# Group norm of a recurrent mixer with eight fused VectorE operations and an early table load, and a new table of how much other work goes into each wait

## The chip, the cores and the metric

The kernel runs on one core of a Trainium2 chip. The metric is the time of one execution on the device in microseconds (us). Engines are called PE (TensorE), VectorE (DVE), ScalarE (ACT), GpSimd (POOL) and SyncE (SP, which issues the DMAs).

## The reference, cut to what matters

One layer over 256 latent tokens of width 1024 with 256 context tokens. A combined input projection feeds two mixers: a recurrence in two directions (8 heads of 64, first over the context, then over the latents) and a windowed attention. Their outputs are projected, gated, merged and projected back; then comes a mixture of 16 experts. The change touches what follows the recurrence:

```python
def rwkv_out(y, r, k, v, lg, r_k, g_lora_b, ln_g, ln_b, out_dtype):
    mu = jnp.mean(y, axis=-1, keepdims=True)                 # per head, over 64
    var = jnp.mean(jnp.square(y - mu), axis=-1, keepdims=True)
    yn = ((y - mu) * lax.rsqrt(var + GN_EPS)).reshape(bsz, t, D_A) * ln_g.astype(f) + ln_b.astype(f)
    bonus = (jnp.sum(r * k * r_k.astype(f), axis=-1, keepdims=True) * v).reshape(bsz, t, D_A)
    g = jax.nn.sigmoid(lg.astype(f)) @ g_lora_b.astype(f)
    return ((yn + bonus) * g).astype(out_dtype)
```

and the router's scores: `scores = sigmoid(t @ router_w)`.

## The kernel before, in words

**Stages in time (profile of before).** Input, modulation and first projections to about 72 us; first preparation (`rw_prep(0)`, decays and products for the context) to 131; first triangular solve (`rw_solve`, 62 small VectorE operations) to 170; first pass (`rw_chain(0)`, 8 rounds over blocks of 32 tokens) to 246; second preparation (`rw_prep(1)`, for the latents) to about 335; second solve to 376; second and last pass (`rw_chain(1)`, rounds 0 to 7) to 437.6; group norm to 454; projections of the two mixers and output projection to 496; router to 502.7; experts to the end.

**Critical work and other work.** The recurrence is a chain of short steps on PE, VectorE and ScalarE with waits between them. The "other work" is one long Python generator, `others()`: value projection, attention, the receptance, the gates, and the projections of the attention's output. `fill()` takes the next number of the list `FILL` (156 numbers, one for each call, the last is 698, "all that is left") and advances the generator by so many steps. Most steps are three matmuls (128x128 weights, 256 columns); the attention's steps are its own pieces, every second or fourth step beside a projection is one of them, and the last two steps of each output group of `gates_b` have 12 matmuls each. Counted through the code the generator has 437 steps: values 65, first attention projection 66, attention of the first half beside the second projection 92, receptance 32, attention of the second half 38, gates 72, `gates_b` 72. `until(name)` advances it until a named point: "v" (66 steps) before the first solve, "r" (256) after the first pass, "att" (294) in the second preparation. Its splits of weights (`split`, L280 on ScalarE, L281 on VectorE) belong to it.

**Order.** The framework's planner puts the instructions of each engine in an order at compile time, from dependencies and its own cost table; among instructions that it takes to be ready, the one that stands earlier in the program goes first. Other work that is ready may therefore be issued ahead of its place in the program when PE would wait. The products in `warm` (L275; bf16, results unused) are kept behind the last matmul of the critical work by edges without a wait, `tc.add_manual_dep(..., ORDERED)`. All DMAs go through SP's queue.

**The group norm** (L1154 to L1184), y being 4 blocks Q of 128x256, in two pairs i:

```python
for i in range(2):
    p = pb(); warm(p, ("gn", i)); mm(p, C["ob"], fl(y, i))            # sum over a head
    V.scalar_tensor_tensor(fl(y, i), p, -1.0 / 64, fl(y, i), ...)     # L1158: y - mean
    S.activation(fl(sq, i), fl(y, i), AF.Square)                      # L1159
fill()
... mm(p, C["obc"], sq) ...; rsqrt(rn.ap, p, 1.0 / 64, 64e-5)         # L285 VectorE, L286 Sqrt, L287 reciprocal
fill()
... pq[Q] = selp x rn, four PSUM banks ...
# then the lines that the change replaces, L1172 to L1176, and for each pair i:
#   five products of warm into a bank freed by the block before, four matmuls (gate),
#   L1181 y * gate (VectorE, PSUM), L1183 cast (ScalarE), L1184 y - cast (VectorE)
```

`rsqrt`'s Sqrt needs another activation table than Tanh and Exp; a table load (ACT_TABLE_LOAD) is put in front of the first activation that needs one. `pb()` and `pa()` hand out PSUM banks, four of each. At the end of the output projection L1272 (VectorE) and L1273 (Sqrt, ScalarE) form the norm of x1, L1275 copies the last quarter of x1 out of PSUM on ScalarE, L1290 forms the scores, L1291 is their Sigmoid, and L1382 a later copy on ScalarE.

Of the kernel before, what the change touches and what calls it, by code (L numbers as in the profile page):

```python
# [13 lines left out]
AF = mybir.ActivationFunctionType  # L14
ALU = mybir.AluOpType
# [103 lines left out]
def _pack(I):  # L119
# [40 lines left out]


FILL = [
# [4 lines left out]
]  # L167
ORDER = [(("k0", 1), ("k1", 0))] * 3

# [63 lines left out]
def hybrid_kernel(ctx: ExitStack, tc: tile.TileContext, a, out, dbg=None, stop=None):  # L233
    nc = tc.nc
    V, S, G, T = nc.vector, nc.scalar, nc.gpsimd, nc.tensor
# [15 lines left out]
    qpool, Q = region("arena_q", NQ, F32R)  # L251
# [5 lines left out]
    def pb(name="pb"):  # L257
        return ps.tile([128, 512], F32, tag="b", name=name, bufs=4)

    own, other = [None], [False]  # L260
    ORDERED = mybir.DependencyInfo(mybir.DependencyClass.NoSync, mybir.DependencyReason.DATA)
# [31 lines left out]
    W = {n: vec[:, o:o + w] for n, (o, w) in _VOFF.items()}  # L293
# [291 lines left out]
    for f in range(2):  # L585
        for q, p in enumerate(fout[f"k{f}"]):
            Q = 2 * f + q
# [276 lines left out]
    vf = A.get(4, 256)  # L864
# [260 lines left out]
    y = A.get(4, 256)  # L1125
# [12 lines left out]
    glb, late, x1 = A.get(512), A.get(128 + NCST[1]), A.get(2, D)  # L1138
# [7 lines left out]
    ssq, rs2, std, junk = A.get(2, 3), A.get(2), A.get(2), A.get(256)  # L1146
    tob = A.get(128)
    sco, sel, gate, gstd, one, oneb, s2 = [A.get(2, 16) for _ in range(7)]
# [2 lines left out]
    pos, over = A.get(2, 16), A.get(2)  # L1151
    ring_grow(A)
    fl = lambda b, i: b[:, 2 * i:2 * i + 2, :].rearrange("p q t -> p (q t)")
    for i in range(2):  # L1154
        p = pb()
        warm(p, ("gn", i))
        mm(p, C["ob"], fl(y, i))
        V.scalar_tensor_tensor(fl(y, i), p, -1.0 / 64, fl(y, i), op0=ALU.mult, op1=ALU.add)  # L1158
        S.activation(fl(sq, i), fl(y, i), AF.Square)  # L1159
# [7 lines left out]
    pq = [pb() for _ in range(4)]  # L1167
    for Q in range(4):
        warm(pq[Q], ("gn", 3), 256)
    for Q in range(4):  # L1170
        mm(pq[Q][:, 0:256], C["selp"][32 * Q:32 * Q + 32, :], rn[32 * Q:32 * Q + 32, :])
    for Q in range(4):  # L1172
        V.tensor_tensor(y[:, Q, :], y[:, Q, :], pq[Q][:, 0:256], op=ALU.mult)
        V.tensor_scalar(y[:, Q, :], y[:, Q, :], W["lng"][:, Q:Q + 1], W["lnb"][:, Q:Q + 1], op0=ALU.mult, op1=ALU.add)
    for i in range(2):
        G.tensor_tensor(fl(y, i), fl(y, i), fl(vf, i), op=ALU.add)  # L1176
        p = pb()
        warm(p, ("gn", 4 + i))
        for q in range(2):
            mm(p[:, q * 256:(q + 1) * 256], glb[:, (2 * i + q) * 128:(2 * i + q + 1) * 128], lg.ap)  # L1180
        V.tensor_tensor(fl(y, i), fl(y, i), p, op=ALU.mult)  # L1181
        yh, yl = ya[i]
        S.copy(yh.r.rearrange("p q t -> p (q t)"), fl(y, i))  # L1183
        V.tensor_tensor(yl.r.rearrange("p q t -> p (q t)"), fl(y, i), yh.ap.rearrange("p q t -> p (q t)"), op=ALU.subtract)  # L1184
# [51 lines left out]
    for n4 in range(4):  # L1236
# [13 lines left out]
        pv = p.rearrange("p (t c) -> p t c", t=2)  # L1250
# [21 lines left out]
    V.scalar_tensor_tensor(std.ap, pss[:, 0:32:16], 1.0 / D, rs2.ap, op0=ALU.mult, op1=ALU.add)  # L1272
    S.activation(std.ap, std.ap, AF.Sqrt)  # L1273
    V.reciprocal(rs2.ap, std.ap)
    S.copy(x1[:, :, 768:1024], pv)  # L1275
    A.put(*wraw, junk, rws)
    P.put(xT)
    ring_grow(P)
# [9 lines left out]

    for tt in range(2):
        V.scalar_tensor_tensor(sco[:, tt, :], plg[tt][:, 0:16], rs2[:, tt:tt + 1], l3.ap, op0=ALU.mult, op1=ALU.add)  # L1290
    S.activation(sco.ap, sco.ap, AF.Sigmoid)  # L1291
    rb = rb.ap.unsqueeze(1).to_broadcast([128, 2, 16])
    V.tensor_tensor(sel.ap, sco.ap, rb, op=ALU.add)

# [213 lines left out]
```

## Time and profile before

| | us |
|---|---|
| median of 3 runs | 741.64 (737.54 to 742.75) |
| profiled execution, its own time | 737.73 |
| its span | 735.9 |
| last pass of the recurrence | 376.0 to 437.6 |
| group norm up to the second split's end | 437.6 to 453.9 |

The span goes from the first to the last instruction; 1.8 us of the execution lie around it. Times in the rows are us from the span's start. "Lnnn" is the line of the kernel; for helpers (`mm` L264, `split` L280 and L281, `rsqrt` L285 to L287) it is the helper's. A wait at the end of a row is the idle time of that engine before the instruction and what ended it.

### The profile page before, as it was taken

What the parts mean: (1) busy time and instruction counts of PE and PEld (TensorE: products, weight loads), DVE (VectorE), ACT (ScalarE), POOL (GpSimd) and SP (SyncE); (2) the same over time, 40 slices, a digit from 0 to 9 for tenths busy, and PEclk for the clock granted to TensorE, in tenths of its full rate; (3) what the DMA queues carried; (4) which work ended last, traced back from release to release, by engine and by line L of the source; (5) the groups of instructions that cost most, each with busy time, mean ns of one, the idle gap of its engine ahead of it and who ended that gap; (6) DMA issues with size and microseconds to landing.
All of it is one profiled execution on the core that took longest, in us unless ns stands there. A gap on an engine that the chain in (4) does not pass through costs nothing.

```text
span 735.9 us, 14592 instructions
## 1 busy us (share of the span) xinstructions
PE 681.6 (93%) x6053; PEld 455.6 (62%) x6059; DVE 397.4 (54%) x738; ACT 301.4 (41%) x604; POOL 101.0 (14%) x90
## 2 busy tenths in 40 slices
PE   4999788999999979689999998998999999999996
PEld 2667677885777844367988766995534544544532
DVE  2445985999774586968975456844213212212113
ACT  5436677447755366845444423432201101101110
POOL 0002354003223044350012201000000000000000
PEclk9999879999999977999999999999999999999999
DMA  9844011231120343777651158969999999999951
GB/s 363 324 168 134 4 59 37 80 107 59 59 63 20 112 147 113 237 262 261 201 193 60 56 197 306 361 245 381 410 408 411 409 410 412 406 411 411 409 220 61
DMA packets 46297, 165.34 MB, mean 225 GB/s; under 512 B 5392, under 2 KB 6800, under 8 KB 45328
## 3 DMA queue, kind: packets, MB, share of 16 engines
q1 hardware_dynamic: 46224, 164.34, 59.9%
q8 instruction: 49, 0.80, 0.4%
q14 instruction: 24, 0.20, 0.1%
HBM read 163.27 MB, written 1.05 MB: 223 GB/s over the span
## 4 chain that ended last, share of the span: by engine, by line
PE 73%; DVE 12%; ACT 9%; issue 2%; DMA 2%; POOL 1%; DVEq 0%; ACTq 0%; POOLq 0%
PE pa L264 53%; PE pb L264 16%; DVE arena_q L281 3%; ACT arena L753 2%; ACT arena L736 1%; PE pb L275 1%; PE pa L967 1%; ACT arena_q L280 1%; DVE arena L696 1%; DVE arena L790 1%; DVE arena L792 1%; DMA arena<-in_modr_dram 1%; DMA arena<-in_pab_dram 1%; DVE arena L693 1%; PE pb L338 1%
## 5 line engine op out<-in xcount | busy, mean ns | idle before, releaser
L264 PE MATMUL pa<-arena_p,arena_q 128*128 128x256 f32 (+1 forms) x984 | 164.3, 314 | 3.3 <-ACT arena_p L373 1.2
L264 PEld LDWEIGHTS pa<-arena_p,arena_q 128*128 128x128 f32 x984 | 134.5, 189 | 24.1 <-issue 5.5
L264 PE MATMUL pa<-arena,arena_m 128*64 128x512 f32 (+1 forms) x652 | 147.1, 555 | 0.0
L264 PE MATMUL pb<-arena 128*32 128x64 f32 (+13 forms) x2248 | 112.0, 270 | 17.7 <-DVE arena L710 5.7
L264 PEld LDWEIGHTS pb<-arena 128*32 128x32 f32 (+7 forms) x2246 | 70.3, 137 | 54.7 <-issue 19.7
L264 PEld LDWEIGHTS pa<-arena,arena_m 128*64 128x64 f32 x652 | 48.5, 137 | 83.7 <-issue 80.3
L280 ACT CAST arena_q<-arena 128x1024 fp32r<-128x1024 f32 (+1 forms) x66 | 62.8, 955 | 80.9 <-PE pa L264 55.1
L281 DVE TENSOR_TENSOR arena_q<-arena,arena_q 128x1024 fp32r<-128x1024 f32 (+1 forms) x66 | 77.6, 1176 | 23.3 <-ACT arena_q L280 18.7
L1408 DVE TENSOR_TENSOR arena_m<-arena_m,pa 128x512 f32<-128x512 f32 x8 | 5.5, 688 | 96.7 <-PE pa L264 96.7
L264 PE MATMUL pa<-arena_q,arena_p 128*128 128x256 f32 x384 | 57.2, 296 | 0.0
L264 PEld LDWEIGHTS pa<-arena_q,arena_p 128*128 128x128 f32 x384 | 49.4, 194 | 6.3 <-issue 3.6
L813 POOL TENSOR_TENSOR arena<-arena 64x512 f32<-64x512 f32 x30 | 32.0, 1068 | 115.6 <-DVE arena L843 113.7
L1349 ACT ACTIVATE arena_m<-pa,arena 128x128 f32<-128x128 f32 x32 | 12.1, 457 | 78.0 <-PE pa L264 78.0
L264 PE MATMUL pa<-arena_p,arena_m 128*64 128x512 f32 x140 | 41.3, 593 | 0.0
L264 PE MATMUL pa<-arena 128*64 128x256 f32 (+5 forms) x192 | 37.8, 446 | 1.7 <-ACT arena L968 1.7
L280 ACT CAST arena_r<-arena_m 128x512 fp32r<-128x512 f32 x16 | 9.9, 618 | 64.9 <-DVE arena_m L1428 64.9
L1428 DVE SCALAR_TENSOR_TENSOR arena_m<-pa,arena,arena_p 128x512 f32<-128x512 f32 x16 | 12.0, 751 | 43.1 <-PE pa L264 43.1
L264 PEld LDWEIGHTS pa<-arena_m,arena 128*128 128x128 f32 x256 | 30.8, 201 | 6.6 <-issue 5.7
L809 ACT COPY arena<-arena 32x256 f32<-32x256 f32 x64 | 25.8, 403 | 18.7 <-PE pb L264 16.8
L264 PE MATMUL pa<-arena_m,arena 128*128 128x128 f32 x256 | 32.3, 287 | 0.9 <-DVE arena_m L1336 0.9
L843 DVE TENSOR_TENSOR arena<-pb,arena 64x512 f32<-64x512 f32 x30 | 20.7, 689 | 15.9 <-PE pb L264 15.4
L264 PE MATMUL pb<-arena,arena 64*64 64x64 f32 (+1 forms) x496 | 26.9, 251 | 0.7 <-ACT arena L829 0.6
(210 smaller groups left out, 846.2 us busy)
## 6 DMA issues: line engine op xcount, KB each, us to landing
arena<-in_w_dram SPq DMA_DIRECT2D x137, 512.0 KB, 9.6
arena<-in_win_dram SPq DMA_DIRECT2D x42, 512.0 KB, 4.0
arena_p<-in_w_dram SPq DMA_DIRECT2D x35, 512.0 KB, 10.1
arena<-in_modr_dram SPq DMA_DIRECT2D x32, 512.0 KB, 4.1
arena<-in_modw_dram SPq DMA_DIRECT2D x4, 2048.0 KB, 14.3
arena<-in_w_dram SPq DMA_DIRECT2D x20, 256.0 KB, 8.2
arena_m<-in_w_dram SPq DMA_DIRECT2D x10, 512.0 KB, 8.8
arena<-in_pab_dram SPq DMA_DIRECT2D x8, 512.0 KB, 3.2
```

The source lines that it names most:

```text
L264: i = T.matmul(out, lhsT, rhs, start=start, stop=stop, skip_group_check=True)
L275: i = T.matmul(p[:, 512 - n:], cb("ob", 128), cb("scanm", n), start=True, stop=True, skip_group_check=True)
L280: S.copy(dhi.bitcast(F32R), src)
L281: eng.tensor_tensor(dlo.bitcast(F32R), src, dhi, op=ALU.subtract)
L338: T.transpose(p[:, (2 * k + i) * 128:(2 * k + i + 1) * 128], xn[:, 2 * st + i, kc * 128:(kc + 1) * 128], ident)
L693: V.tensor_tensor_scan(cum[:, go], C["scanm"], sg[:, go], 0.0, op0=ALU.mult, op1=ALU.add)
L753: (V.tensor_copy if h and c2 else S.copy)(BT[f][64 - 64 * h:128 - 64 * h, d, q, c2:8:2, :], pv[64 * c2:64 * c2 + 64, :, h, :])
L809: S.copy(Z[rv, h, :, d, :], vt[32 * c4:32 * c4 + 32, h, tt, :, :])
L813: G.tensor_tensor(sd[r_], Z[r_, h], pc[r_, :, :, i].rearrange("p d q -> p q d").unsqueeze(3) .to_broadcast([64, 4, 2, 64]), op=ALU.mult)
L843: V.tensor_tensor(Z1[r_, h], pyv[r_], sd[r_], op=ALU.add)
L1349: S.activation(dst, src, AF.Identity, scale=m4[:, kc:kc + 1], bias=m3[:, kc:kc + 1])
L1428: V.scalar_tensor_tensor(sil.ap, py[n2], gsl[pr % 2].ap, m5r[:, n2 * 512:(n2 + 1) * 512], op0=ALU.mult, op1=ALU.mult)
```

## The change

Two activations stand ahead of the group norm; the scale and shift of each block are two `scalar_tensor_tensor` operations on VectorE, (y * ln_g) * rstd and (y + ln_b) + bonus, done for each pair of blocks inside the loop over pairs, and GpSimd's additions are gone; the copy L1275 is ordered behind the Sigmoid of the scores on ScalarE, by an edge without a wait; `FILL` has other numbers.

```diff
+    S.activation(std[:, 0:1], y[:, 0, 0:1], AF.Square)
+    S.activation(std[:, 0:1], std[:, 0:1], AF.Sqrt)
     for i in range(2):
         p = pb()
         warm(p, ("gn", i))
...
-    for Q in range(4):
-        V.tensor_tensor(y[:, Q, :], y[:, Q, :], pq[Q][:, 0:256], op=ALU.mult)
-        V.tensor_scalar(y[:, Q, :], y[:, Q, :], W["lng"][:, Q:Q + 1], W["lnb"][:, Q:Q + 1], op0=ALU.mult, op1=ALU.add)
     for i in range(2):
-        G.tensor_tensor(fl(y, i), fl(y, i), fl(vf, i), op=ALU.add)
+        for Q in (2 * i, 2 * i + 1):
+            V.scalar_tensor_tensor(y[:, Q, :], y[:, Q, :], W["lng"][:, Q:Q + 1], pq[Q][:, 0:256], op0=ALU.mult, op1=ALU.mult)
+        for Q in (2 * i, 2 * i + 1):
+            V.scalar_tensor_tensor(y[:, Q, :], y[:, Q, :], W["lnb"][:, Q:Q + 1], vf[:, Q, :], op0=ALU.add, op1=ALU.add)
         p = pb()
         warm(p, ("gn", 4 + i))
...
-    S.copy(x1[:, :, 768:1024], pv)
+    x1_last = S.copy(x1[:, :, 768:1024], pv)
...
-    S.activation(sco.ap, sco.ap, AF.Sigmoid)
+    scored = S.activation(sco.ap, sco.ap, AF.Sigmoid)
+
+    tc.add_manual_dep(x1_last.ins, scored.ins.name, ORDERED, reason="not before")
```

The numbers of `FILL` that differ, each with the wait that it belongs to (counted through the calls of `fill()`):

| where | old | new |
|---|---|---|
| first preparation: third wait of the products (half 0, direction 1); turn of half 0, direction 0 | 4; 0 | 3; 3 |
| first solve: after columns 21; 27 | 2; 2 | 1; 0 |
| first pass: round 3, start; round 4, second wait | 0; 0 | 3; 2 |
| second preparation: last turn of half 0, ahead of `until("att")` | 1 | 6 |
| second preparation, half 1: after the second decay; second and third wait of the products (direction 1) | 1; 3, 4 | 0; 2, 3 |
| second solve: after column 5 | 2 | 1 |
| last pass, round 0: third wait | 3 | 5 |
| round 1: second, third, fourth wait | 0, 2, 2 | 2, 3, 3 |
| round 2: second, third | 2, 7 | 3, 6 |
| round 5: second, third, fourth | 1, 6, 2 | 2, 9, 3 |
| round 6: second, third | 2, 10 | 3, 16 |
| round 7: second | 6 | 1 |

The sum without the last number is 312 in the old list and 330 in the new one.

## Rows read from the trace of the kernel before

**Rows 1.** The page, part 1 (busy time of each engine, its share of the span, and its instructions) and, of part 2 (40 slices of 18.4 us, busy tenths), PE and the clock granted to it.
```profile
PE 681.6 (93%) x6053; PEld 455.6 (62%) x6059; DVE 397.4 (54%) x738; ACT 301.4 (41%) x604; POOL 101.0 (14%) x90
...
PE   4999788999999979689999998998999999999996
...
PEclk9999879999999977999999999999999999999999
```

**Rows 2.** Stretches of the span, all engines: start and end, length, busy us and number of instructions of PE, weight loads, VectorE, ScalarE and GpSimd; then the granted clock (1.00 is 2.4 GHz), the DMA share and GB/s.
```profile
104.00:131.00 27.00, 23.26 (x291) 19.68 (x290) 16.95 (x29) 21.38 (x47) 12.57 (x11) 0.99 0.13 40
292.00:324.00 32.00, 25.10 (x268) 15.61 (x266) 28.38 (x42) 20.86 (x45) 14.34 (x12) 1.00 0.73 240
340.00:376.00 36.00, 34.23 (x306) 31.89 (x304) 33.34 (x72) 15.43 (x23) 0.00 (x0) 1.00 0.66 207
376.00:437.60 61.60, 59.99 (x1143) 47.94 (x1148) 32.41 (x55) 24.94 (x59) 12.88 (x13) 1.00 0.31 107
437.60:451.20 13.60, 11.04 (x63) 6.23 (x64) 8.17 (x18) 3.57 (x5) 2.79 (x3) 1.00 0.92 365
451.20:494.00 42.80, 42.54 (x365) 41.61 (x365) 28.76 (x42) 17.73 (x31) 0.16 (x1) 1.00 0.84 306
```

**Rows 3.** VectorE in order of time in the group norm: start, us, engine, line, operation, output<-input and shape, xcount, and in brackets the idle time before it and what ended it. Neighbours with one line are merged, so x2 with 0.75 is two of 0.41 that overlap.
```profile
436.44 1.23 DVE L281 TENSOR_TENSOR arena_q<-arena,arena_q 128x1024 fp32r<-128x1024 f32 x1 [0.23 <-ACT arena_q L280]
437.58 0.48 DVE L860 TENSOR_TENSOR arena<-arena,pb 128x128 f32<-128x128 f32 x2
...
443.08 0.42 DVE L285 TENSOR_SCALAR arena<-pb 128x256 f32<-128x256 f32 x1 [1.39 <-PE pb L264]
...
446.65 0.75 DVE L1173 TENSOR_TENSOR arena<-arena,pb 128x256 f32<-128x256 f32 x2 [0.79 <-PE pb L264]
...
449.86 0.67 DVE L1181 TENSOR_TENSOR arena<-arena,pb 128x512 f32<-128x512 f32 x1
...
453.19 0.69 DVE L1184 TENSOR_TENSOR arena_p<-arena,arena_p 128x512 fp32r<-128x512 f32 x1 [0.69 <-ACT arena_p L1183]
```

**Rows 4.** ScalarE in the same stretch.
```profile
440.07 0.63 ACT L1159 ACTIVATE arena<-arena 128x512 f32<-128x512 f32 x1 [3.66 <-DVE arena L1158]
441.73 0.63 ACT L1159 ACTIVATE arena<-arena 128x512 f32<-128x512 f32 x1 [1.03 <-DVE arena L1158]
442.37 1.28 ACT L286 ACT_TABLE_LOAD   x1
443.67 0.42 ACT L286 ACTIVATE arena<-arena 128x256 f32<-128x256 f32 x1
...
452.54 0.62 ACT L1183 CAST arena_p<-arena 128x512 fp32r<-128x512 f32 x1 [1.35 <-DVE arena L1181]
```

**Rows 5.** GpSimd, then PE, in the same stretch (L275 are the products of `warm`, L264 all others).
```profile
448.20 1.27 POOL L1176 TENSOR_TENSOR arena<-arena 128x512 f32<-128x512 f32 x1 [8.34 <-DVE arena L1174]
...
447.13 1.24 PE L275 MATMUL pb<-arena 128*128 128x512 bf16 x4 [0.49 <-DVE arena L1173]
448.20 1.03 PE L264 MATMUL pb<-arena 128*128 128x256 f32 x4
...
450.15 1.03 PE L264 MATMUL pb<-arena 128*128 128x256 f32 x4
```

**Rows 6.** VectorE's groups by line and shape: output<-input, xcount | busy us in all, mean ns of one | idle before. The last row is line 1174 by itself: duration in ns, least/median/most.
```profile
L1253 DVE SCALAR_TENSOR_TENSOR arena_p<-pa,arena,arena_p 128x256 f32<-128x256 f32 x8 | 3.9, 483 | 5.9 <-PE pa L264 5.9
...
L1110 DVE SCALAR_TENSOR_TENSOR arena<-arena 128x256 f32<-128x256 f32 x4 | 1.8, 481 | 3.5 <-ACT arena L924 3.5
...
L1174 DVE TENSOR_SCALAR arena<-arena x4: 399/407/983, 447.3 to 449.5; 128x256 f32<-128x256 f32 x4
```

**Rows 7.** ScalarE behind the last output projection, then one row of VectorE and one of PE there.
```profile
495.98 0.59 ACT L1275 COPY arena<-pb 128x512 f32<-128x512 f32 x1 [1.17 <-PE pb L1262]
496.52 0.20 ACT L1273 ACTIVATE arena<-arena 128x2 f32<-128x2 f32 x1
...
498.03 0.23 ACT L1291 ACTIVATE arena<-arena 128x32 f32<-128x32 f32 x1
499.93 0.37 ACT L1382 COPY arena_p<-pa 128x256 f32<-128x256 f32 x1 [1.66 <-PE pa L264]
...
496.32 0.16 DVE L1272 SCALAR_TENSOR_TENSOR arena<-pb,arena 128x2 f32<-128x2 f32 x1 [2.28 <-PE pb L264]
...
502.73 1.60 PE L264 MATMUL pa<-arena_m,arena 128*128 128x128 f32 x11 [0.86 <-DVE arena_m L1336]
```

**Rows 8.** One row of PE ahead of the second preparation (72 matmuls of the other work without a break); then, of PE, only the matmuls into PSUM tiles pa, which in these stretches are the other work: stretch, length, busy us (xcount), clock, DMA.
```profile
245.80 8.80 PE L264 MATMUL pa<-arena_p,arena_q 128*128 128x256 f32 x72
...
376.00:437.60 61.60, 24.50 (x142) 1.00 0.31 107
423.00:437.60 14.60, 5.76 (x31) 1.00 0.46 160
```

**Rows 9.** Stretches with low clock, and one with PE mostly idle, columns as in rows 2.
```profile
260.00:272.00 12.00, 7.88 (x55) 3.21 (x54) 11.89 (x20) 8.38 (x19) 4.74 (x4) 0.71 0.49 176
272.00:284.00 12.00, 12.00 (x97) 6.28 (x96) 6.90 (x15) 5.85 (x13) 7.50 (x5) 0.50 0.26 87
304.00:308.00 4.00, 1.41 (x16) 0.89 (x16) 3.68 (x8) 3.18 (x9) 2.67 (x3) 1.00 0.81 238
```

8 rows, old and new, of the table FILL are left out of this document.

## The prediction

> **What bounds the kernel now.** I read the page first. TensorE (PE) is busy 93% of the span and no other engine passes 54% [rows 1]; but its line of the 40 slices has two dips, and those with the granted clock below 9 are where the kernel loses time. Next I cut the span into stretches [rows 2]. Four of them matter here. In the last pass of the recurrence (376 to 437.6) PE has 59.99 of 61.6 us of work, so it is full up to 1.6 us. In the preparation of that pass (292 to 324) it has 25.10 of 32, VectorE 28.38: there VectorE is the bound and PE idles 6.9 us. In the first preparation (104 to 131) PE idles 3.7 us. In the group norm (437.6 to 451.2) PE has 11.04 of 13.60, much of it the bf16 products of `warm`, and no engine is full: that is a chain of latencies. After it PE is full again (42.54 of 42.80 up to 494), so whatever the group norm ends earlier, the end of the kernel comes earlier by as much. The chain that ended last goes through the group norm's own instructions, one engine after the other [rows 3 to 5].
>
> **The change, part by part.**
>
> *Early root.* Square and Sqrt of one column, behind the last write of y, pull the table load ahead. Now the second Square ends at 442.36, the load of 1.28 us runs 442.37 to 443.65 and Sqrt starts at 443.67; its operand, VectorE's L285, is there at 443.08 + 0.42 = 443.50 [rows 3, 4]. Without the load Sqrt could start some 0.03 later than 443.50, so the load costs 0.14 us, not 1.28: most of it lies beside PE and L285 already. The two new instructions (0.20 each, as L1273 [rows 7]) and the load take about 1.7 us from the end of L860 at 438.06, to 439.75; ScalarE's next work is the first Square at 440.07 [rows 4]. So they are hidden, by 0.3 us; if that cover were gone, the first Square would be late by what is over. Gain 0.14.
> The Trainium skill ("ScalarE: Activation LUTs", What ACT_TABLE_LOAD costs) puts a drain of about 1.38 us beside a load of 1.283. By it the early root would be worth some 1.5 us instead of 0.14. The row has the load right behind Square and Sqrt right behind the load, so the sum goes without it.
>
> *Scale and shift.* Removed: four products with PSUM (L1173, 0.41 us; two of them take 0.75, so one starts 0.34 behind the other), four tensor_scalars (L1174, 0.40, one of them 0.98) and two GpSimd additions of 1.27 us with a handover at each end [rows 3, 5, 6]. Added: eight scalar_tensor_tensor of 128x256. The nearest rows are L1253 with a PSUM operand (0.483) and L1110 in SBUF alone (0.481) [rows 6]; with the overlap of L1173 one starts every 0.41. Pair 0 is then through at 446.65 + 3 x 0.41 + 0.48 = 448.4, where GpSimd's sum now comes at 448.20 + 1.27 = 449.47. But L1181 also wants the gate product in PSUM: five warm products wait for the first bank, then four matmuls end at 448.20 + 1.03 = 449.23, or 0.07 later since a 0.48 frees the bank instead of a 0.41. So pair 0's L1181 starts at 449.3 and not at 449.86. For pair 1 the same queue of PE ends at 450.15 + 1.03 + 0.07 = 451.25 [rows 5]. From there L1181 0.68, the cast 0.62, L1184 0.69 with some 0.03 between [rows 3, 4]: 453.34, where the trace has 453.88. That is 0.54. What is late next is thus PE's own queue of warm and gate products. If VectorE lets pair 0's L1184 in ahead of pair 1's L1181, it is about 453.55: 0.33. I take 0.45, between them.
> The Trainium skill ("VectorE: DVE Perf Modes", the perf-mode tier table) speaks against this part: an fp32 tensor_scalar in SBUF goes at twice the rate of an operation with two tensors, 1227 against 2293 ns for 2048 elements. An estimate by it is 0.13 us more for each of four operations, 0.5 in all; the rows differ by 0.48 - 0.40 = 0.08, 0.3 in all. By the page the gain is 0.25, since VectorE would then end it and not PE.
>
> *The copy behind the scores.* L1275 stands on ScalarE ahead of L1273 now, 495.98 to 496.57. L1273 starts at 496.52 and its operand comes from VectorE's L1272 at 496.32 + 0.16 = 496.48 [rows 7]. The copy costs at most 0.04. Behind the sigmoid (498.26) it ends at 498.9, the next on ScalarE behind it is L1382 at 499.93, and the first product that reads x1 starts at 502.73 [rows 7], so it is covered by 1.0 and 3.8 us. I count 0.
>
> *The amounts of other work.* The code has 437 steps of other work. A step is three matmuls of the large products at 8.80 / 72 = 0.122 us [rows 8], 0.37 us a step. `until` makes the number of steps equal again at three places, so a shift lives only up to the next one. Laid side by side, the new list gives: two steps more in the first preparation (one fewer in a product wait, three more in the turn), taken back by the first `until`; three fewer in the first solve and five more in the first pass, taken back by the second; five more ahead of `until("att")`, taken back there; then three fewer in the products of the second preparation, one fewer in the solve, and in the rounds of the last pass shifts that grow to 14 steps more in round 6, 9 at the end.
> For the rounds of the last pass the trace decides. From 376 on, PE still runs 142 matmuls of the other work [rows 8], which is the last 36 steps; by the old list 87 steps should be left. In the last two rounds 31 are run [rows 8], under 5 steps, where the list leaves 33. The planner had fetched other work far ahead of its place, and the lead is some 50 steps at the start of the pass and 28 at round 6. A list that asks for up to 14 steps earlier asks for work that has been done. So the rounds get 0, though they hold most of the changed numbers. The same holds in the first pass: the burst in front of the second preparation is 72 matmuls, 24 steps, where the list leaves 107.
> Left are the preparations. In the first, two steps (0.7 us) move into a wait where PE idles: between -0.7 and, if they stand ahead of the products, +0.7; I take -0.3. In the second, three steps (1.1 us) leave the queue ahead of the products of a stretch that VectorE bounds: between -1.1 and +1.1 (they come back in the solve, where VectorE is busy 33.34 of 36 [rows 2]); I take -0.5.
>
> **Sum.** -0.14 - 0.45 - 0 - 0.8 = -1.4 us. The profiled execution took 737.73 us (span 735.9 and 1.8 around it) and would become 736.3; it lies 3.9 below the median of the runs. On the median 741.64 the forecast is 740.2. A measurement tells about 1% from no change here, 7.4 us, and that is five times the forecast gain.
>
> **Rivals.**
> A, *the idle PE is filled.* PE idles 3.7 + 6.9 + 1.6 = 12.2 us in the stretches in which numbers change [rows 2]. If half of it goes, the gain is 6.1 and 0.6 from the group norm: 735. For it: that much idle time is there, and all of the order is laid anew by the planner. Against it: in 292 to 324 VectorE has 28.38 of 32 us and the steps' own splits (1.2 us each on VectorE, L281 [rows 3]) come on top.
> B, *slower: a new low-clock stretch.* In 272 to 284 PE is granted 1.2 GHz and not 2.4, after it had been idle for 4.1 of 12 us in 260 to 272 [rows 9]. The second preparation is the place: it loses three steps, and PE already sits idle 6.9 of 32 us there at full clock. If that fall comes a second time with PE full for some 12 us at half rate, as in 272 to 284 [rows 9], 6 us are lost: 741.6 - 0.6 + 6 = 747. It decides as soon as the granted clock in 292 to 324 is below 1.00. Against it: 304 to 308 has PE busy only 1.41 of 4 and the clock stayed.
> C, *nothing*: the gains of 0.6 are taken back by the planner's new order; 741.6.
>
> **How the numbers follow.** Forecast 0.5, A 0.25, B 0.15, C 0.1. The forecast's own range is 737.5 to 742.5 (bounds above, and the runs shown spread by 5 us). For 8 in 10 it reaches three quarters of the way into A's idle time (0.6 + 9.2: 732) and to 746 on B's side. Faster by over 1% (below 734.2) is half of A: 0.13. Slower by over 1% (above 749.1) needs B with a longer stretch: 0.07. The rest, 0.80, is within 1%.
>
> **What would show it.** Right: no table load between L285's operand and Sqrt, one between L860 and the first Square; no GpSimd work behind 440; from the start of the first 128x256 operation to the end of the second split some 6.7 us where it is 7.2; the eight operations at 0.48; the last pass within 2 us of its 61.6; PE full behind the group norm. Wrong: the last pass shorter or longer by more (then the list does bind there), a different clock in 260 to 324, or a solve whose length changes by over 1 us.

## The result, and the profile after

The changed kernel takes 735.76 us (median of 20 runs, 731.89 to 738.47), the kernel before 738.94 beside it on the same chip (20 runs): ratio 0.9934 [0.9913, 0.9955], that is 4.9 us less; the two medians by themselves lie 3.2 us apart. The forecast was a gain of 1.4. The time is below the forecast's own range (737.5 to 742.5) and inside the one given for 8 in 10 (732 to 746). The two profiled executions differ by much less (737.02 and 737.73): that of after lies above its median and that of before below its own, so what follows compares stretches, not spans.

The page, busy time by engine and granted clock, answers to [rows 1]:

```profile
PE 681.8 (93%) x6053; PEld 457.9 (62%) x6059; DVE 395.7 (54%) x738; ACT 301.1 (41%) x606; POOL 101.3 (14%) x88
...
PEclk9999959999999967999999999999999999999999
```

Of the gain nothing is to be seen there. A ledger by landmarks of the chain shows where the two executions part (VectorE's instructions, ends of stretches in us):

| stretch | before | after | difference |
|---|---|---|---|
| start to the end of the first solve (L795 starts) | 169.32 | 171.11 | +1.8 |
| to the first decay scan of the second preparation (L693) | 92.63 | 87.61 | **-5.0** |
| second preparation and second solve | 113.22 | 112.27 | -1.0 |
| last pass, to the last L860 | 62.41 | 62.11 | -0.3 |
| group norm, to the second split's end | 16.30 | 19.17 | **+2.9** |
| the rest | 282.0 | 282.9 | +0.9 |

The first row is not of the change: seven other kernels below that share the list of after, or its first numbers, have 167.3 to 170.4 there, and the clock in 75 to 171 differs (0.89 here, 0.93 before). The second and the fifth are what has to be explained: a gain in the first pass that no step of the forecast had, and a loss in the group norm, where the forecast had its safest gains. The stretches that answer to [rows 2, 9], set to the landmarks of after (columns as there):

```profile
104.00:131.00 27.00, 25.55 (x313) 22.94 (x310) 15.06 (x26) 20.52 (x42) 13.30 (x11) 0.87 0.14 41
292.00:324.00 32.00, 25.46 (x274) 16.71 (x275) 28.22 (x39) 20.59 (x43) 14.74 (x10) 0.95 0.69 232
335.80:371.80 36.00, 33.61 (x305) 31.19 (x305) 33.49 (x72) 14.77 (x23) 0.00 (x0) 1.00 0.68 217
371.80:433.10 61.30, 60.41 (x1165) 49.51 (x1168) 32.17 (x55) 26.29 (x61) 12.88 (x13) 1.00 0.33 106
433.10:449.60 16.50, 12.94 (x65) 7.15 (x66) 9.91 (x19) 3.98 (x7) 0.48 (x1) 0.90 0.96 357
449.60:494.00 44.40, 44.40 (x377) 42.80 (x376) 28.27 (x42) 17.94 (x32) 0.00 (x0) 1.00 0.75 274
260.00:272.00 12.00, 7.17 (x91) 3.83 (x91) 11.95 (x20) 7.94 (x17) 7.13 (x5) 0.68 0.55 192
```

The last pass is as long as it was, PE is full behind the group norm, and the clock in 292 to 324 is 0.95 where it was 1.00. In the group norm it is 0.90. VectorE there, against [rows 3]:

```profile
433.10 0.49 DVE L860 TENSOR_TENSOR arena<-arena,pb 128x128 f32<-128x128 f32 x2 [0.64 <-PE pb L264]
433.50 1.22 DVE L281 TENSOR_TENSOR arena_q<-arena,arena_q 128x1024 fp32r<-128x1024 f32 x1
434.96 0.69 DVE L1161 SCALAR_TENSOR_TENSOR arena<-pb,arena 128x512 f32<-128x512 f32 x1 [0.24 <-PE pb L264]
438.11 0.23 DVE L1235 CAST arena<-arena 128x128 bf16<-128x128 f32 x1 [2.45 <-DMA arena<-in_late_dram]
...
438.38 0.68 DVE L1161 SCALAR_TENSOR_TENSOR arena<-pb,arena 128x512 f32<-128x512 f32 x1
440.46 0.42 DVE L285 TENSOR_SCALAR arena<-pb 128x256 f32<-128x256 f32 x1 [1.39 <-PE pb L264]
...
443.90 0.87 DVE L1177 SCALAR_TENSOR_TENSOR arena<-arena,pb 128x256 f32<-128x256 f32 x2 [0.79 <-PE pb L264]
444.69 0.88 DVE L1179 SCALAR_TENSOR_TENSOR arena<-arena 128x256 f32<-128x256 f32 x2
445.48 0.87 DVE L1177 SCALAR_TENSOR_TENSOR arena<-arena,pb 128x256 f32<-128x256 f32 x2
446.27 0.88 DVE L1179 SCALAR_TENSOR_TENSOR arena<-arena 128x256 f32<-128x256 f32 x2
447.69 0.69 DVE L1184 TENSOR_TENSOR arena<-arena,pb 128x512 f32<-128x512 f32 x1 [0.55 <-PE pb L264]
...
451.58 0.69 DVE L1187 TENSOR_TENSOR arena_p<-arena,arena_p 128x512 fp32r<-128x512 f32 x1 [0.69 <-ACT arena_p L1186]
```

Two casts of late constants (L1235 and L1236; L1232 and L1233 before) stand in VectorE's queue between the two mean subtractions, and the first waits 2.45 us for its load. The constants are wanted only behind the group norm, but the second subtraction is queued behind the cast: it comes 3.42 us behind the first, where the kernel before has 1.72, with the casts in the same place and no wait:

```profile
439.28 0.69 DVE L1158 SCALAR_TENSOR_TENSOR arena<-pb,arena 128x512 f32<-128x512 f32 x1 [1.22 <-PE pb L264]
439.89 0.22 DVE L1232 CAST arena<-arena 128x128 bf16<-128x128 f32 x1
...
441.00 0.69 DVE L1158 SCALAR_TENSOR_TENSOR arena<-pb,arena 128x512 f32<-128x512 f32 x1 [0.76 <-PE pb L264]
```

ScalarE, against [rows 4]:

```profile
433.62 0.20 ACT L1155 ACTIVATE arena<-arena 128x1 f32<-128x1 f32 x1 [0.87 <-DVE arena L860]
433.84 1.28 ACT L1156 ACT_TABLE_LOAD   x1
435.13 0.20 ACT L1156 ACTIVATE arena<-arena 128x1 f32<-128x1 f32 x1
435.69 0.63 ACT L1162 ACTIVATE arena<-arena 128x512 f32<-128x512 f32 x1 [0.35 <-DVE arena L1161]
439.10 0.63 ACT L1162 ACTIVATE arena<-arena 128x512 f32<-128x512 f32 x1 [2.78 <-DVE arena L1161]
440.91 0.42 ACT L286 ACTIVATE arena<-arena 128x256 f32<-128x256 f32 x1 [1.18 <-DVE arena L285]
```

The load has moved ahead and is covered; Sqrt starts 0.03 behind the end of its operand (440.46 + 0.42 = 440.88), where it was 0.17. And PE, in stretches of 2 us:

```profile
444.00:446.00 2.00, 1.51 (x5) 0.98 (x6) 2.00 (x6) 0.00 (x0) 0.00 (x0) 0.82 1.03 418
446.00:448.00 2.00, 2.00 (x6) 1.18 (x6) 1.45 (x4) 0.00 (x0) 0.00 (x0) 0.50 0.97 393
448.00:450.00 2.00, 2.00 (x10) 1.23 (x8) 1.08 (x2) 0.62 (x1) 0.00 (x0) 0.83 0.87 311
```

Behind that wait PE falls to the lower of its two levels (1.2 GHz) while it is at the gate's products. So the eight new operations (two of them take 0.87 together) end in front of a PE that is late (0.55 ahead of L1184). Of the 2.9 us that the norm is longer, the later subtraction is 1.7 and the clock most of the rest; whether the wait also brought the clock down is asked in experiment 3. The load that the cast waits for, after:

```profile
430.21 0.33 SPq L396 DMA_DIRECT2D arena<-in_pab_dram  x1
432.93 0.33 SPq L1141 DMA_DIRECT2D arena<-in_late_dram  x1
```

and in the kernel before, where L396 has gone ahead at 428.01:

```profile
436.37 0.33 SPq L1141 DMA_DIRECT2D arena<-in_late_dram  x1
```

From issue to landing it took 5.15 us after and 2.93 before. From issue until VectorE stands at the cast there are 2.72 us after (435.65) and 3.52 before (439.89): a split of 1.2 us (L281) that stood ahead of the last L860 now comes behind it. So in the kernel before the load landed 0.6 us ahead of the cast. The order of SP alone doesn't set the landing: with SP's order of before the same load took 3.2 us in experiment 2, 4.6 in 5 and 5.5 in 9. What sets it stays open.

### The profile page after: what moved, and what is told of

Its sections match the earlier page's. It is cut to its first block, busy times and chain, and to the rows that moved or that the text cites. A ratio compares the mean times of both kernels' runs of the same rounds, so it can differ in the third digit from the quotient of the medians.

```text
span 735.2 us, 14594 instructions
## 1 busy us (share of the span) xinstructions
PE 681.8 (93%) x6053; PEld 457.9 (62%) x6059; DVE 395.7 (54%) x738; ACT 301.1 (41%) x606; POOL 101.3 (14%) x88
## 3 DMA queue, kind: packets, MB, share of 16 engines
HBM read 163.27 MB, written 1.05 MB: 223 GB/s over the span
## 4 chain that ended last, share of the span: by engine, by line
PE 72%; DVE 15%; ACT 6%; DMA 2%; issue 2%; POOL 0%; DVEq 0%; SPq 0%; ACTq 0%
PE pa L264 51%; PE pb L264 17%; DVE arena_q L281 2%; DVE arena L792 2%; DVE arena L790 2%; ACT arena L753 1%; PE pb L275 1%; ACT arena L736 1%; PE pa L967 1%; ACT arena_q L280 1%; DVE arena L693 1%; DVE arena L696 1%; DMA arena<-in_late_dram 1%; DMA arena<-in_x_dram 1%; DVE arena L705 1%
## 5 line engine op out<-in xcount | busy, mean ns | idle before, releaser
L264 PE MATMUL pa<-arena_p,arena_q 128*128 128x256 f32 (+1 forms) x984 | 162.1, 312 | 7.7 <-DVE arena_q L281 2.7
L264 PEld LDWEIGHTS pa<-arena_p,arena_q 128*128 128x128 f32 x984 | 133.8, 188 | 28.2 <-issue 4.8
L264 PE MATMUL pa<-arena,arena_m 128*64 128x512 f32 (+1 forms) x652 | 148.8, 561 | 0.0
L264 PE MATMUL pb<-arena 128*32 128x64 f32 (+13 forms) x2248 | 113.9, 273 | 12.7 <-DVE arena L710 4.5
L264 PEld LDWEIGHTS pa<-arena,arena_m 128*64 128x64 f32 x652 | 48.9, 138 | 85.0 <-issue 81.0
L264 PEld LDWEIGHTS pb<-arena 128*32 128x32 f32 (+7 forms) x2246 | 72.0, 140 | 47.5 <-issue 17.6
L281 DVE TENSOR_TENSOR arena_q<-arena,arena_q 128x1024 fp32r<-128x1024 f32 (+1 forms) x66 | 75.1, 1138 | 25.7 <-ACT arena_q L280 18.2
L264 PE MATMUL pa<-arena_q,arena_p 128*128 128x256 f32 x384 | 59.2, 304 | 0.0
L264 PEld LDWEIGHTS pa<-arena_q,arena_p 128*128 128x128 f32 x384 | 51.5, 202 | 5.5 <-issue 2.8
L813 POOL TENSOR_TENSOR arena<-arena 64x512 f32<-64x512 f32 x30 | 34.8, 1161 | 115.2 <-DVE arena L843 113.3
L264 PE MATMUL pa<-arena_p,arena_m 128*64 128x512 f32 x140 | 41.3, 593 | 0.0
L264 PE MATMUL pa<-arena 128*64 128x256 f32 (+5 forms) x192 | 35.8, 447 | 1.7 <-ACT arena L968 1.7
L264 PEld LDWEIGHTS pa<-arena_m,arena 128*128 128x128 f32 x256 | 29.2, 192 | 6.6 <-issue 5.7
L264 PE MATMUL pa<-arena_m,arena 128*128 128x128 f32 x256 | 30.7, 278 | 0.9 <-DVE arena_m L1341 0.9
L264 PE MATMUL pb<-arena,arena 64*64 64x64 f32 (+1 forms) x496 | 26.0, 249 | 0.6 <-DVE arena L829 0.4
```

Of the source, the lines that this page charges most:

```text
L264: i = T.matmul(out, lhsT, rhs, start=start, stop=stop, skip_group_check=True)
L281: eng.tensor_tensor(dlo.bitcast(F32R), src, dhi, op=ALU.subtract)
L813: G.tensor_tensor(sd[r_], Z[r_, h], pc[r_, :, :, i].rearrange("p d q -> p q d").unsqueeze(3) .to_broadcast([64, 4, 2, 64]), op=ALU.mult)
```

## The experiments

Each ratio is against the kernel before on the same chip. "First stretch" is from the end of the first solve to the first scan of the second preparation, the second row of the ledger.

**1. The list alone.** The kernel before with the new numbers of `FILL`, no line of code changed.

> The kernel before with the new list alone. By the traces (the list works: the last round of the first pass comes 3.0 us earlier than before, that of the last pass 5.2 us earlier): 0.993 to 0.995 of before, and the last round of the last pass near 427. By the prediction (the list is worth 0.8 us): 0.999, the last round of the last pass within 1.5 us of 432. By a third theory, that a wait for the late constants eats the gain: the pass 5 us shorter, but a gap of VectorE of some 2 us between the two mean subtractions, and 0.996 to 0.999.

735.66 us, 0.9948 [0.9919, 0.9977]. First stretch 87.60, group norm 17.75, with a wait for the late constants and the clock at 1.00:

```profile
436.37 0.23 DVE L1232 CAST arena<-arena 128x128 bf16<-128x128 f32 x1 [2.11 <-DMA arena<-in_late_dram]
```

The list carries the gain, and here it has the wait too.

**2. The code alone.** The changed kernel with the old numbers.

> The changed kernel with the old list: early root, eight fused operations, copy behind the scores. By the prediction: 0.6 us, 0.999 of before, and from the first 128x256 operation to the end of the second split 6.7 us against 7.2. By the theory that the code carries the gain: 0.994. By the theory that PE's own queue of warm and gate products is the limit: that stretch at 6.7, not below.

738.95 us, 0.9989 [0.9960, 1.0017]; first stretch 92.51, group norm 16.13. The code is worth nothing that can be told from zero. Its VectorE from the first 128x256 operation to the second split:

```profile
446.29 0.87 DVE L1177 SCALAR_TENSOR_TENSOR arena<-arena,pb 128x256 f32<-128x256 f32 x2 [0.79 <-PE pb L264]
...
448.65 0.88 DVE L1179 SCALAR_TENSOR_TENSOR arena<-arena 128x256 f32<-128x256 f32 x2
449.44 0.68 DVE L1184 TENSOR_TENSOR arena<-arena,pb 128x512 f32<-128x512 f32 x1
...
452.78 0.69 DVE L1187 TENSOR_TENSOR arena_p<-arena,arena_p 128x512 fp32r<-128x512 f32 x1 [0.69 <-ACT arena_p L1186]
```

The stretch is 453.47 - 446.29 = 7.18 us, 7.23 before (8.37 in after, at the lower clock); the forecast said 6.7. The planner puts all eight operations ahead of pair 0's product with the gate, so L1184 starts at 449.44 with no wait: VectorE's own queue ends it, 3.15 us from the first operation, and not PE.

**3. The casts moved away.** The changed kernel with the two casts ordered behind the last split of the group norm:

```diff
-    V.tensor_copy(trib, C["tri"])
-    V.tensor_copy(onesb, C["ones"])
+    for cast in (V.tensor_copy(trib, C["tri"]), V.tensor_copy(onesb, C["ones"])):
+        tc.add_manual_dep(cast.ins, ya_last.ins.name, ORDERED, reason="not before")
```

> The changed kernel, with the two casts of the late constants ordered behind the group norm on VectorE, and nothing else moved. If the wait of 2.45 us for the late constants in the changed kernel's trace is typical, and PE's fall to half clock behind it comes from it: 3 us faster than the changed kernel, 0.989 to 0.990 of before; the group norm (last addition into y to the end of the second split) falls from 19.2 us to some 15.8, and the clock in it is 1.00. If the wait is an accident of the profiled execution: 0.993, as the changed kernel.

733.03 us (732.02 to 734.46), 0.9901 [0.9863, 0.9940]; group norm 16.22 where after has 19.17, the granted clock stays at 1.00 there, and of all engines only VectorE's order changed. In these two executions the 2.9 us go with the wait. The intervals of this kernel and of after still overlap, and not all of the 2.9 can be put down to the wait. Experiments 1 and 4 have it (2.11 and 2.23 us) at full clock, and their norm takes 17.75 and 17.83: the wait alone is worth some 1.5 us. That it brings the clock down is not shown: of the five kernels with a wait of over 0.9 us the clock is low in the norm in two (after and 9), and of the nine without it in five (6, 7, 10, 11 and 12, the last with the casts moved away).

**4. Without the early root.** The changed kernel without the two added activations.

> The changed kernel without the two early activations. By the rows the load then stands between the second Square and Sqrt and costs 0.14 us: 0.994, the same as the changed kernel, Sqrt 0.1 to 0.2 us later behind its operand than with the early root. By the rule of a drain beside the load: 1.5 us slower, 0.996.

736.02 us, 0.9936 [0.9903, 0.9969], the same as after. From L285 to the first 128x256 operation 3.57 us, with the root 3.44: worth 0.13 us, as far as a trace shows it.

**5. Two numbers.** The kernel before with only the two changed numbers of the first preparation (4 to 3 and 0 to 3).

> The kernel before with only two numbers changed, both in the first preparation (third product wait 4 to 3, turn 0 to 3). The numbers of the first pass's rounds and of its solve left as they were; changed alone they leave every instruction of VectorE, ScalarE and the DMAs in its place. If these two numbers carry the list's gain: 0.993 to 0.996 of before, the last round of the first pass near 235 (before 240.5), the reciprocal of 3.33 us ahead of the first copy of its round and not between its two copies, and no wait for the late constants. By the prediction: 0.9996. If the gain is from the second preparation or the last pass: 1.000.

735.50 us, 0.9941 [0.9910, 0.9972]; first stretch 87.63. Two of the 23 changed numbers give as much as the whole list, within the intervals, and they stand a stage ahead of where it appears. The wait for the late constants is here too, with the old numbers of the last pass: 0.99 us.

**6. The second preparation.** The kernel before with the three lower numbers there (1 to 0, 3 to 2, 4 to 3).

> The kernel before with only the three numbers of the second preparation that lose a step each. By the prediction: 0.5 us, 0.999 to 1.000. By rival B (a low-clock stretch in it): slower, and a clock below 1.00 in 292 to 324. By the theory that the first preparation carries all: 0.998 to 1.002, the second solve's end within 1.5 us of before.

738.52 us, 0.9964 [0.9930, 0.9998]; second preparation and solve 110.93 (113.22 before). The last pass is shorter by 2.2 us (60.17) and the group norm longer by 4.4 (20.70): 27 more matmuls of the other work now run in the norm, and the casts come later and don't wait. Something is gained; the size is not settled: over all kernels here with the old numbers preparation and solve take 112.2 to 115.2 us, with the new ones 110.3 to 116.0, and much of that is when the clock comes back (0.84 to 1.00 in 292 to 324). The second solve by itself does separate: 38.4 to 39.9 us from its first to its last transposition in the eight kernels with these three numbers, 40.8 to 41.5 in the six without.

**7. The last pass.** The kernel before with the new numbers of its rounds only.

> The kernel before with only the numbers of the last pass. By the prediction: 1.000. If the rounds bind: the last pass (end of the second solve to the last addition into y) is shorter than 62.0 by 1 to 2 us. If the list's wait for the late constants comes from these numbers (they move that load behind a 512 KB and a 1 MB one): a gap on VectorE of 1 to 2.5 us ahead of the casts and 1.001 to 1.003.

742.51 us, 1.0024 [0.9996, 1.0053]; last pass 63.08 (62.41 before). The rounds, which hold most of the changed numbers, bring nothing.

**8. Pair 0 first.** Experiment 3 with pair 1's first products ordered behind pair 0's product with the gate, so that VectorE doesn't do all eight first.

```diff
-            V.scalar_tensor_tensor(y[:, Q, :], y[:, Q, :], W["lng"][:, Q:Q + 1], pq[Q][:, 0:256], ...)
+            scaled = V.scalar_tensor_tensor(y[:, Q, :], y[:, Q, :], W["lng"][:, Q:Q + 1], pq[Q][:, 0:256], ...)
+            if i:
+                tc.add_manual_dep(scaled.ins, gated.ins.name, ORDERED, reason="not before")
```

(`gated` is pair 0's product with the gate, L1184 of the changed kernel.)

> The changed kernel with the casts behind the group norm, and pair 1's fused operations ordered behind pair 0's gate product on VectorE. From the first 128x256 operation to the end of the second split it takes 7.18 us in the run with the casts alone. By the prediction's step (PE's own queue of warm and gate products sets the start of both gate products): 6.65 to 6.9. If VectorE's eight operations were not what held pair 0: 7.2. If VectorE's work in all sets the end: 7.2 to 7.5.

One run, 733.72 us. From the first operation to the second split's end 7.70 us, not less: pair 0's product now starts 2.67 us from the first operation, as the forecast had it (2.65), but it waits 1.01 us for PE and VectorE stands idle through it, then pair 1's four operations come late. The order that the planner chose was the better one.

By then I held that the first stretch was long because of one piece of other work: in the fourth round of the first pass the attention's reciprocal (L287, 3.33 us) stands on VectorE between the round's two copies (L829) in the kernel before, and ahead of them with the new list; that round takes 14.88 us before and 10.98 in experiment 1. Two runs put this to the test.

**9. The reciprocal behind the copies.** The kernel before, one edge added.

```diff
-        rsqrt(rk[0:64], p[0:64, :], 1.0 / 64, 1e-6)
+        rcp = rsqrt(rk[0:64], p[0:64, :], 1.0 / 64, 1e-6); g and tc.add_manual_dep(rcp.ins, AT_[103].ins.name, ORDERED, reason='x')
```

(`AT_[103]` is the last copy of that round; `rsqrt` returns its reciprocal.)

> The kernel before, its own list, and one edge without a wait: the 3.33-us reciprocal of the attention's keys (L287, 64x512), which stands on VectorE between the two VectorE copies (L829) of the fourth round of the first pass (203.42 and 208.83), goes behind the second of them. Up to that place the order of every engine is the same as before. Theory, the place of this piece of other work in a round makes the first pass long: the second copy comes about 3.3 us earlier (some 205.5), the round from its L821 to the next (14.88 before) falls to some 11.5 to 13, since the reciprocal then stands ahead of L843 and takes part of it back; first solve's end to last L821 of the first pass 68 to 69.5 where it was 71.14 and 66.38 with the new list; ratio 0.996 to 0.998. Rival, what shortens the first pass is where the matmuls of other work lie on PE: the first pass stays within 0.7 of 71.1, ratio 0.999 to 1.001.

741.68 us, 1.0029 [0.9999, 1.0059]. The round did get shorter, to 13.58, and the copies came early:

```profile
205.67 0.42 DVE L829 COPY arena<-pb 32x256 f32<-32x256 f32 x1
206.12 3.35 DVE L287 RECIPROCAL arena<-arena 64x512 f32<-64x512 f32 x1
209.50 1.41 DVE L843 TENSOR_TENSOR arena<-pb,arena 64x512 f32<-64x512 f32 x2
...
213.27 0.42 DVE L821 TENSOR_SCALAR arena<-pb 128x256 f32<-128x256 f32 x1 [1.05 <-PE pb L264]
```

The rounds behind it got longer, and the first stretch is 91.71, 0.9 less than before. (The group norm of this run has the wait for the late constants, 1.92 us, so the stretch says more here than the ratio.)

**10. The reciprocal cut short.**

```diff
-        V.reciprocal(dst, dst)
+        last = V.reciprocal(dst[:, 0:64] if short else dst, dst[:, 0:64] if short else dst); return last
...
-        rsqrt(rk[0:64], p[0:64, :], 1.0 / 64, 1e-6)
+        rsqrt(rk[0:64], p[0:64, :], 1.0 / 64, 1e-6, g == 1)
```

> The kernel before with the same reciprocal formed of 64 of the 512 columns only (the rest of the keys' norms are left without it), so that 3.33 us become about 0.5; all else as before up to that place. Theory (place of the reciprocal): the first pass falls by 2.8 to 4, to 67 to 68.3, that is most of the way to the 66.4 of the new list, although no number of the list is changed. Rival (PE's matmuls): within 0.7 of 71.1.

One run, 741.42 us; what this kernel leaves out is the norms of most of the keys. The chain itself is faster even than the theory had it: from the end of the solve to the last L821 of the first pass 64.37 us, where before has 71.14 and experiment 5 has 66.40. And it gains next to nothing:

```profile
171.16:235.53 64.37, 63.38 (x904) 45.78 (x904) 43.47 (x78) 43.55 (x93) 21.39 (x21) 1.00 0.17 55
235.53:262.62 27.09, 27.09 (x247) 20.60 (x246) 13.58 (x25) 12.82 (x27) 0.35 (x1) 1.00 0.23 79
```

The other work that the shorter rounds did not take is done behind them (27.09 us, 21.49 before), with PE full throughout: first stretch 91.46. The code wants all of it up to the point "r" in front of the second preparation. So a shorter pass is not what shortens the stretch. My theory fell on that, although the length of the pass that it gave as its sign was reached and passed; the rival, PE, stands.

**11. Both preparations.** The kernel before with five numbers: those of 5 and of 6.

> The kernel before with five numbers of the new list: the two of the first preparation (alone 0.9941) and the three of the second (alone 0.9964). Theory, the two gains lie in different stretches (first pass; second preparation and second solve) and add: ratio 0.989 to 0.992, first pass 66.4, second decay to second solve's end 111 where it was 113.2. Rival, the planner's order of the second preparation is laid anew by the first change already and the second gives nothing on top: 0.993 to 0.996, 113 or more.

730.50 us (728.69 to 735.81), 0.9896 [0.9856, 0.9937], the lowest of all here. First stretch 87.61. By the ratio the two gains add (0.9941 x 0.9964 = 0.9905); that they do is not shown, since the interval overlaps that of experiment 5. The profiled execution fits the rival: second preparation and solve 113.17, as before, with the clock at 0.86 in 292 to 324. Only the solve itself is shorter there too (38.46, before 41.35).

**12. The same five, with the code and the moved casts.**

> The changed code with the casts of the late constants behind the last split of the group norm (as in the third experiment), and of the new list only those five numbers, the old ones elsewhere. Theory, gains add and the numbers of the last pass bring nothing: 0.985 to 0.989, below the 0.9901 of the third experiment. Rival, they don't add: 0.989 to 0.993; if it is above 0.993 the numbers of the last pass did carry part of the gain.

734.23 us, 0.9916 [0.9884, 0.9947], in the range of the rival. Not below 11: the code of the change adds nothing to the five numbers that can be told from zero. First stretch 89.13, with the clock at 0.98 in it. The group norm takes 20.47 us here and 20.55 in 11, with the 27 more matmuls of experiment 6 in both; in 11 the casts don't wait, so moving them had nothing to take away.

## What made the first stretch shorter

The whole stretch in one row, first of the kernel before:

```profile
169.32:261.95 92.63, 91.56 (x1150) 66.74 (x1149) 60.78 (x103) 56.83 (x120) 21.79 (x21) 1.00 0.19 61
```

then of experiment 5:

```profile
167.73:255.36 87.63, 86.67 (x1145) 65.01 (x1143) 58.31 (x104) 55.26 (x119) 23.65 (x21) 1.00 0.21 65
```

and of after:

```profile
171.11:258.72 87.61, 86.65 (x1145) 65.01 (x1143) 58.34 (x103) 55.23 (x119) 23.64 (x21) 1.00 0.21 65
```

In all three PE idles about 1 us, so PE is the bound; and nearly the same matmuls (1150 and 1145) at the same clock take 91.56 us in one and 86.67 in the other. Full is not a fixed amount of work. Two forms carry most of it (forms overlap on PE, so their differences do not add up to the 4.89 us exactly); in the kernel before

```profile
L264 PE MATMUL pa<-arena_p,arena_q 128*128 128x512 f32 x30 | 9.3, 422 | 0.0
L264 PE MATMUL pa<-arena 64*128 64x512 f32 x20 | 8.2, 636 | 0.0
```

and in experiment 5

```profile
L264 PE MATMUL pa<-arena_p,arena_q 128*128 128x512 f32 x25 | 7.3, 415 | 0.0
L264 PE MATMUL pa<-arena 64*128 64x512 f32 x20 | 6.0, 636 | 0.0
```

The first form, 2.0 us: five products were done earlier, ahead of the end of the solve. In the solve PE is full (38.26 of 38.32 us from 131 on before, 36.70 of 36.73 in experiment 5). In the first preparation it idles less than it did, 2.76 us in 104 to 131 where [rows 2] have 3.74:

```profile
104.00:131.00 27.00, 24.24 (x289) 21.05 (x289) 16.22 (x30) 23.09 (x49) 12.98 (x9) 1.00 0.13 41
```

So some 1 us of these products fills idle time. Whether the rest is paid for ahead of the stretch can't be told: up to the end of the solve the kernels with the two numbers take 167.3 to 171.1 us, those without 166.8 to 171.2. The second form, 2.2 us, is the same 20 matmuls. They are the attention's scores, in groups of four: two for each of two heads, one head with its 64 rows in one half of the array and the other in the other half. On PE of the kernel before:

```profile
188.56 1.12 PE L264 MATMUL pa<-arena 64*128 64x512 f32 x2
189.61 0.64 PE L264 MATMUL pb<-arena 128*32 128x64 f32 x28
190.19 1.12 PE L264 MATMUL pa<-arena 64*128 64x512 f32 x2
```

and of experiment 5:

```profile
182.98 1.13 PE L264 MATMUL pa<-arena 64*128 64x512 f32 x4
```

Side by side the two heads take 1.13 us together. With the chain's products between them they take 1.12 each. The starts alone say the same: PE's next product begins 1.06 us behind the start of the four (184.04) and 1.05 behind that of each two (189.61, 191.24). That split is there twice in the kernel before (also around 203.7, with two products of the chain between) and not at all with the new numbers: 2 x 1.1 = 2.2 us. So it is in all 14 kernels here: both splits and a first stretch of 91.5 to 92.6 us in the six with the old pair of numbers, no split and 87.6 to 89.1 in the eight with the new one. The other forms give the rest, each by some tenths (128x128 of L967 from 5.9 to 5.3, 128*64 from 5.4 to 5.0). The Trainium skill ("TensorE: Matmul & The Clock Gate", The mechanism, on packing small matmuls) says that matmuls on different row groups run concurrently and that matmuls are not reordered. The first is what these rows show; the second fits them, since PE did not bring the two heads' products together over the 0.58 us that lay between them at 189.61. Experiment 10 fits too: its 64x512 take 8.2 us as before, and its gain of 1.2 is a pair of 32x512 that came to stand together (2.2 to 1.1 us). That neighbours decide the 2.2 us is read from the rows of two orders; a run that moves only this pair was not made.

## Why the prediction was right or wrong, step by step

That the time fell inside the range for 8 in 10 was luck as far as the sum goes: nearly all of the gain came through a term that it had at 0.3, and by a mechanism that it did not have.

- *First preparation, -0.3:* the step that failed. "Two steps (0.7 us) move into a wait" priced the numbers by the amount of work that they move. PE does idle 1.0 us less there, but the two numbers are also the difference between two orders of PE's work through the whole first pass, worth 5.0 us in the trace and 4.4 by the ratio of experiment 5. The bounds of 0.7 on either side were too narrow for the same reason.
- *"So PE is full up to 1.6 us":* read rightly, but taken as fixed work. It hid that a full stretch can become shorter.
- *The rounds of both passes, 0:* right in sum (experiment 7: 1.0024). In the first pass the argument by the lead held: experiments 1 and 5 differ in the numbers of the first solve and pass and of all later stages, and up to 295 us the order of every engine is the same in both but for two matmuls at 147. In the last pass (experiment 7) PE's order is that of before up to 429.2; from there 14 matmuls of the other work come up to 5 us earlier, in the last two rounds, to no gain.
- *Second preparation, -0.5:* right in sign; experiment 6 has 0.9964, which is 2.7 us with a wide interval, and experiments 5 and 11 differ by 0.0045 with intervals that overlap. That the steps "come back in the solve, where VectorE is busy" did not cost: the second solve is shorter by 2.3 us in after (39.06, before 41.35). That was one of the signs of being wrong, and so was the clock in 292 to 324.
- *Early root, -0.14:* 0.13 (experiment 4). No drain beside the load is to be seen, as the row of before had it.
- *Scale and shift, -0.45:* 0.05 (experiment 2). Durations and PE's queue were right; the failed step is "pair 0's L1181 starts at 449.3", which took for granted that VectorE would do pair 0 first. Eight operations, 3.15 us, stand ahead of it instead.
- *The wait that nobody priced:* the sum named what the table load and the copy would collide with, but not the load of the late constants, which in the kernel before landed only 0.6 us ahead of its cast (436.37 + 2.93 = 439.30, the cast at 439.89). After, VectorE is at the cast at 435.65 and the load lands at 432.93 + 5.15 = 438.08. Experiments 5 and 9, with the old numbers of the last pass, have the wait too (0.99 and 1.92 us): it is a matter of a narrow margin, not of the list alone. The wait and the lower clock together cost 2.9 us in this execution, the wait by itself some 1.5.
- *Rival A (idle PE filled, 735):* right number, another mechanism in the main. Of the 5.0 us, 2.0 are products done earlier, some 1.0 of that in idle time; the rest is PE time that is no longer needed. *Rival B:* its condition came (292 to 324 at 0.95), its price did not: 32 x 0.05 x 2 = 3.2 us at half rate and not 12, so 1.6 us lost and not 6. In experiment 11 that stretch is at 0.86, some 9 us at half rate, and the kernel is still the lowest.
- *The copy behind the scores, 0:* nothing to be seen; not run by itself.

Left open: why the planner's order falls out so much better with the two new numbers than with the old ones. It is one of many orders, and no rule of the numbers is shown.

## What to carry to other kernels

A stretch in which the profile shows the engine full can still be shortened without taking work out: compare the same forms of matmul in two orders, and look for products on halves or quarters of the array that stand apart. A number in a scheduler's list is not worth the work that it moves; it chooses an order, and its effect may appear a stage later. Before a chain is changed, look for loads that land only tenths of a microsecond ahead of their use, and keep what waits for them out of the engine's queue ahead of the chain's own work.

## What was not expected of the hardware

- Two heads' products on the two halves of the array: 1.13 us together, 1.12 us each when 28 other matmuls, or only 2, stand between them.
- Nearly the same idle time went with either level of the clock. After, PE idles 1.56, 1.34 and 0.55 us in the group norm behind the wait, and in 446 to 448 it is granted 1.2 GHz; in experiment 1 it idles 1.15, 1.47 and 0.49 and the clock stays at 1.00. In experiment 10 it idles 1.47 and 0.49, as before, and the clock falls (0.90 in the norm).
- A faster chain can be worth little: 6.8 us less in the first pass (experiment 10), 1.2 us less at the end of the same stretch.
